# The down projection of a hybrid decoder step, its order written by hand and its last two column tiles taken together in three token parts

## Chip, cores and metric

The kernel runs on one core of one Trainium2 chip. A time is the device time of one execution in microseconds (us). The core has five engines that work beside each other: TensorE (PE; its loads of the stationary operand are listed as PEld), VectorE (DVE), ScalarE (ACT), GpSimd (POOL) and SyncE (SP), which here only issues DMAs. The profile takes one execution apart by instruction.

## The reference, cut to what matters

The kernel is one step of a one-layer decoder trunk for a prompt of 512 tokens and 8 single sample tokens, which are worked on together as 520 columns. The change concerns the last part of the layer:

```python
x = layer_norm(ALPHA * x + mixed @ w_out, ln1_g, ln1_b)         # D_MODEL = 1024
g, u = jnp.split(x @ w_gate_up, 2, axis=-1)                     # D_FF = 2816
ffn = (jax.nn.silu(g) * u) @ w_down                             # (520 x 2816) @ (2816 x 1024)
ple = jax.nn.sigmoid(x @ w_ple_gate) * (p @ w_ple)
x = layer_norm(ALPHA * x + ffn + ple, ln2_g, ln2_b)             # y_prompt, y_sample
```

## The kernel before

Activations are kept with the features on the 128 partitions and the 520 tokens as columns: 8 sample tokens first, then 512 prompt tokens. A matrix product in float32 accuracy is made of three products of rounded parts: each weight and each activation is split into a part hi and a remainder lo, and hi x hi, hi x lo and lo x hi are summed in PSUM. A weight piece is split by two instructions in `split` (L215): a copy to hi on ScalarE (L216) and a subtraction for lo on VectorE (L217).

Weights come through three rings. `add_block` registers blocks of a weight matrix in the order of use, each cut into pieces. `load_next` (DMA at L163, on SyncE's queue) brings a block into one of two `raw` buffers of 128 x 2048. `prep_next` splits the next piece into the rings `whi` and `wlo` of three buffers each, or into a place named in `dest`; when a block's last piece is split, the next load is issued. `get(k)` prepares pieces up to k + 2 and hands out piece k.

The down projection has 8 output tiles of 128 features (f = 0 to 7) and 22 blocks of 128 along D_FF (k). In the kernel before, tiles 0 to 5 are made in three pairs (b); for each pair there are three groups of k (8, 8 and 6) and two pieces, one per tile, so 18 pieces. `mm3ab` (matmuls at L243) takes each piece against both token halves, 264 and 256 columns, in two PSUM banks: for each k and each of the three products two matmuls follow each other with the same stationary weights. Tile 6 has three pieces of its own and the same form. Tile 7 is made by halves: first `mm3` (L226) for the 264 columns, then `mmb` (L1843) for the 256 columns.

Beside this runs the end of the layer. `mkbase(f)` forms ALPHA * x + ple for tile f: per half, two loads that SyncE issues (L1748 for the saved tanh `th`, from a ring of three, and L1749 for the saved `ple` product) and three VectorE instructions (L1750 to L1752). A finished half tile is added to its base from PSUM (`ev_d`, L1776), transposed to tokens on partitions by two TensorE transposes (`ev_dt`, L1785), copied to the row buffer R2 by ScalarE (L1786), and its statistics are taken by VectorE (`ev_ds`, L1794).

Around tiles 0 to 6 the order of instructions on each engine is the framework's: it simulates a timeline and picks. From the second half of tile 7 on, the order is written out by hand (`tc.manual_schedule` for TensorE, VectorE, GpSimd and ScalarE; the DMA queue of SyncE is left to the framework). In that last part the tokens of chunks 0 and 1 are normalised while `mmb` runs, those of chunks 2 and 3 after it: per chunk of 128 tokens the mean and variance (L1858, L1859), a power on GpSimd (L1860), then centering times gain (L1867) and scaling plus shift (L1871) on VectorE; for three quarters of the second chunk of each pair it is a normalisation on ScalarE (L1875), the gain on GpSimd (L1879) and the shift on VectorE (L1883). Stores are issued at L1887. The 8 sample tokens are normalised with their features on partitions (L1902 to L1928), transposed at L1940 and stored.

Of the kernel before, what the change touches and what calls it, by code (L numbers as in the profile page):

```python
# [17 lines left out]
P = 128  # L18
D = 1024
KD = D // P  # L20
NS = 8
# [24 lines left out]
def rr(ap):  # L46
    return ap.bitcast(F32R)
# [3 lines left out]
def tile_hybrid_step(  # L51
# [25 lines left out]
    def psm():  # L77
        return pm.tile([P, 512], F32, tag="m", name=nm("psm"))
# [7 lines left out]
    def ring(tag, n, bufs, p=P):  # L86
        return wp.tile([p, n], F32, tag=tag, name=nm(tag), bufs=bufs)
# [3 lines left out]
    def slab(i):  # L91
        return up.tile([P, U], F32, tag=f"T{i}", name=nm(f"T{i}_"))
# [94 lines left out]
    def prep_next():  # L187
        i = state["prep"]
        if i >= len(pieces):
            return  # L190
        state["prep"] += 1
        bi_, a, kc, pcol, last = pieces[i]
# [5 lines left out]
        split(hi, lo, raws[bi_][:, :, a : a + pcol], G if i in pool_lo else V)  # L198
        ready[i] = (hi, lo)
        if last:  # L200
            raws.pop(bi_)
            load_next()
# [1541 lines left out]
    def mkbase(f):  # L1744
        for hf, (c0, n) in enumerate(HALVES):
            th = ring("th", 264, 3)[:, :n]
            bs = base(f, hf)
            nc.sync.dma_start(th, thsc[:, f, c0 : c0 + n])  # L1748
            nc.sync.dma_start(bs, plesc[:, f, c0 : c0 + n])  # L1749
            V.scalar_tensor_tensor(bs, th, 1.0, bs, ALU.add, ALU.mult)  # L1750
# [19 lines left out]
    def dpart(g, w):  # L1770
        return [(w[0], w[1], 0, KG[g][1], hhi[g], hlo[g], 0)]
# [24 lines left out]
    kp = k_dn  # L1796
    for b in range(3):
        pps = [(psm(), psm()) for _ in range(2)]
        cnt = [0, 0]
        for g in range(3):  # L1800
            for a in range(2):
                w = get(kp)
                kp += 1
                i = 6 * b + 2 * g + a
                for j in range(2 * i, 2 * i + 2) if i < 3 else ():
                    split(hhi[2][j], hlo[2][j], h6[j])
                for j in bases.get(i, ()):
                    mkbase(j)
                if i == 12:
                    late_rows()  # L1810
                cnt[a] = mm3ab(pps[a], dpart(g, w), total=3 * KF, begin=cnt[a])
                if g == 2:
                    if "R2" not in late_r:
                        late_r["R2"] = slab(2)[:, : NCH * D].rearrange("p (c d) -> p c d", c=NCH)
                    for hf in range(2):
                        f = 2 * b + a
                        ev_ds(f, hf, ev_dt(f, hf, ev_d(f, hf, pps[a][hf])))
    pp = (psm(), psm())
    cnt = 0
    for g in range(3):  # L1820
        w = get(kp)
        kp += 1
        cnt = mm3ab(pp, dpart(g, w), total=3 * KF, begin=cnt)
    for hf in range(2):
        ev_ds(6, hf, ev_dt(6, hf, ev_d(6, hf, pp[hf])))
    pa, pb = psm(), psm()
    ws = []
    cnt = 0
    for g in range(3):
        ws.append(get(kp, 1))  # L1830
        kp += 1
        cnt = mm3(pa, HALVES[0], dpart(g, ws[g]), total=3 * KF, begin=cnt)

    R2 = late_r["R2"]
    ysm, l2g, l2b, RQ, rss = (late_r[n] for n in ("ysm", "g", "b", "RQ", "rss"))
    h0, h1, q3 = slice(0, 512), slice(512, D), slice(768, D)

    def mmb(k0, k1):
        for k in range(k0, k1):
            g, j = k // 8, k % 8  # L1840
            hi, lo = ws[g]
            for i, (w, x) in enumerate(((hi, hhi), (hi, hlo), (lo, hhi))):
                T.matmul(  # L1843
                    pb[:, :256], rr(w[:, j, :]), rr(x[g][j][:, 264:NT]),
                    start=(k == 0 and i == 0), stop=(k == KF - 1 and i == 2),
                )

    class Out:
        def __init__(self, c):
            self.c = c  # L1850
            self.mv = ring("mv2", 4, 2).rearrange("p (k a) -> p k a", k=2)
            self.rs = ring("rs2", 2, 2)
            self.nb = ring("nb", 1, 2)
            self.r = [R2[:, c + i, :] for i in range(2)]

        def stats(self):
            for i in range(2):
                V.bn_aggr(self.mv[:, i, :], st2[:, self.c + i])  # L1858
            V.tensor_scalar(self.rs, self.mv[:, :, 1], LN_EPS, None, ALU.add)  # L1859
            G.tensor_tensor(self.rs, self.rs, nhalf[:, :2], ALU.pow)  # L1860

        def neg(self):
            V.scalar_tensor_tensor(self.nb, self.mv[:, 1, 0:1], -1.0, self.rs[:, 1:2], ALU.mult, ALU.mult)

        def center(self, i, cs):
            s = self.r[i][:, cs]
            V.scalar_tensor_tensor(s, s, self.mv[:, i, 0:1], l2g[:, cs], ALU.subtract, ALU.mult)  # L1867

        def scale(self, i, cs):
            s = self.r[i][:, cs]  # L1870
            V.scalar_tensor_tensor(s, s, self.rs[:, i : i + 1], l2b[:, cs], ALU.mult, ALU.add)  # L1871

        def norm(self, a):
            s = self.r[1][:, a : a + 256]
            S.activation(s, s, AF.Identity, bias=self.nb, scale=self.rs[:, 1:2])  # L1875

        def gain(self, a):
            s = self.r[1][:, a : a + 256]
            G.tensor_tensor(s, s, l2g[:, a : a + 256], ALU.mult)  # L1879

        def shift(self, a):
            s = self.r[1][:, a : a + 256]
            V.tensor_tensor(s, s, l2b[:, a : a + 256], ALU.add)  # L1883

        def store(self, i, cs, eng=nc.sync):
            t0 = (self.c + i) * P
            eng.dma_start(y_prompt[0, t0 : t0 + P, cs], self.r[i][:, cs])  # L1887
# [7 lines left out]
    E = mybir.EngineType  # L1895
    with tc.manual_schedule(engines={E.PE, E.DVE, E.Pool, E.Activation}):
        oa, ob = Out(0), Out(2)
        r2a = ev_d(7, 0, pa)
        mmb(0, 4)
        psa = ev_dt(7, 0, r2a)  # L1900
        pst = pss()
        T.matmul(pst[:, :64], onesD, RS.rearrange("p f b -> p (f b)"), start=True, stop=True)  # L1902
        mmb(4, 10)
# [3 lines left out]
        ev_ds(7, 0, psa)  # L1907
        oa.stats()
        T.matmul(pst[:, 64:128], onesD, RQ.rearrange("p f b -> p (f b)"), start=True, stop=True)
        mmb(10, KF)  # L1910
        oa.center(0, h0)
        V.tensor_reduce(rss[:, 1], pst[:, 64:128].rearrange("p (f b) -> p b f", f=KD), axis=AX.X, op=ALU.add)
        V.tensor_scalar(rss[:, 1], rss[:, 1], LN_EPS, None, ALU.add)
        G.tensor_tensor(rss[:, 1], rss[:, 1], nhalf[:, 0:1].to_broadcast([P, NS]), ALU.pow)
        oa.neg()
        for a in range(0, 768, 256):
            oa.norm(a)
            oa.gain(a)
        oa.scale(0, h0)
        oa.store(0, h0)  # L1920
        oa.center(0, h1)
        oa.scale(0, h1)
        oa.store(0, h1)
        oa.center(1, q3)
        oa.shift(0)
# [3 lines left out]
        r2b = ev_d(7, 1, pb)  # L1929
        psb = ev_dt(7, 1, r2b)  # L1930
        oa.scale(1, q3)
        oa.shift(256)
        oa.store(1, h0)
        oa.shift(512)
        oa.store(1, h1)
        ev_ds(7, 1, psb)
        ob.stats()
# [6 lines left out]
        ob.center(0, h0)  # L1944
        ob.neg()
        for a in range(0, 768, 256):
            ob.norm(a)
        for a in range(0, 768, 256):
            ob.gain(a)
        ob.scale(0, h0)  # L1950
        ob.store(0, h0)
        ob.center(1, q3)
        ob.scale(1, q3)
        ob.center(0, h1)
        ob.shift(0)
        ob.scale(0, h1)
        ob.store(0, h1)
        ob.shift(256)
        ob.store(1, h0, nc.scalar)
        ob.shift(512)  # L1960
        ob.store(1, h1)
# [33 lines left out]
```

## Time and profile before

| | us |
|---|---|
| median of 3 runs | 891.84 |
| lowest and highest run | 890.12, 892.92 |
| the profiled execution | 894.93 |
| its span, first to last instruction | 892.9 |

The profile is of one execution; its span is 2.0 us shorter than its time. Rows of the profile give times from the start of the span. The granted clock is that of TensorE, as a share of 2.4 GHz.

### The profile page before, as it was taken

The numbers are of one execution on the slowest core, as the hardware profiler recorded it, in microseconds if no ns is written. First come the engines' busy times: TensorE is split into PE (matmuls) and PEld (weight loads), VectorE is DVE, ScalarE is ACT, GpSimd is POOL, SyncE is SP. The second block draws the span as 40 slices with busy tenths as digits, with TensorE's granted clock in tenths as the row PEclk, the third lists the DMA queues.
The fourth block names the chain that finished last, engine by engine and source line by source line (L and its number), as shares of the span: only waits on it lengthen the run. The fifth ranks groups of instructions, "written<-read, shape, count | busy, mean of one in ns | idle before, by whom it ended". The sixth has DMA issues, their size and how long they took to land.

```text
span 892.9 us, 18610 instructions
## 1 busy us (share of the span) xinstructions
PE 866.8 (97%) x7082; PEld 854.0 (96%) x7082; DVE 658.9 (74%) x1591; ACT 480.6 (54%) x1138; POOL 160.5 (18%) x320
## 2 busy tenths in 40 slices
PE   8899999999999999999999999999999999999994
PEld 7899899999999899999999999999999999999993
DVE  6797655688878777778877879899988875824327
ACT  5545354657777655557426646666666565212212
POOL 4441321115364411311013200000000000000004
PEclk9999999999999999999999999999999999999997
DMA  7543631336465451121610223334333348641212
GB/s 241 176 156 104 170 122 54 56 120 149 144 177 162 143 142 49 50 93 48 231 54 1 73 85 105 107 96 118 107 96 107 108 123 255 197 161 61 69 40 96
DMA packets 128089, 103.69 MB, mean 116 GB/s; under 512 B 7242, under 2 KB 123682, under 8 KB 127976
## 3 DMA queue, kind: packets, MB, share of 16 engines
q1 hardware_dynamic: 127856, 102.25, 38.4%
q8 instruction: 55, 0.90, 0.4%
q14 instruction: 34, 0.28, 0.1%
q10 hardware_dynamic: 144, 0.26, 0.1%
HBM read 91.14 MB, written 12.47 MB: 116 GB/s over the span
## 4 chain that ended last, share of the span: by engine, by line
PE 77%; DVE 10%; DMA 5%; ACT 3%; issue 2%; POOL 1%; SPq 1%; DVEq 0%; ACTq 0%; POOLq 0%
PE psm L243 36%; PE psm L1600 14%; PE pss L1600 10%; PE psm L226 6%; DMA big<-vsd 2%; DVE wlo L217 1%; PE pss L736 1%; PE psm L467 1%; PE pss L683 1%; PE pss L720 1%; PE psm L1428 1%; DMA thsc<-gt 1%; DMA wdb<-bcd 1%; ACT T L1371 1%; PE pss L1069 1%
## 5 line engine op out<-in xcount | busy, mean ns | idle before, releaser
L243 PE MATMUL psm<-T,whi 128*128 128x264 f32 (+1 forms) x1744 | 304.3, 286 | 0.7 <-DVE Qbd L670 0.4
L243 PEld LDWEIGHTS psm<-T,whi 128*128 128x128 f32 x1744 | 248.5, 188 | 2.9 <-issue 0.8
L243 PE MATMUL psm<-T,wlo 128*128 128x256 f32 (+1 forms) x928 | 203.2, 288 | 2.0 <-DVE wlo L217 2.0
L217 DVE TENSOR_TENSOR wlo<-raw,whi 128x1024 fp32r<-128x1024 f32 (+1 forms) x78 | 94.6, 1213 | 76.0 <-ACT whi L216 75.3
L243 PEld LDWEIGHTS psm<-T,wlo 128*128 128x128 f32 x928 | 147.8, 188 | 3.1 <-DVE wlo L217 2.5
L216 ACT ACTIVATE whi<-raw 128x1024 fp32r<-128x1024 f32 (+1 forms) x78 | 80.6, 1035 | 120.6 <-PE psm L243 108.4
L1778 POOL COPY amaskA<-tmp 128x8 f32<-128x8 f32 x8 | 1.7, 207 | 372.7 <-DVE tmp L1776 372.7
L708 POOL TENSOR_SCALAR g<-g,sm 128x256 f32<-128x256 f32 (+1 forms) x64 | 36.4, 582 | 80.5 <-DVE sm L706 24.1
L1584 DVE TENSOR_TENSOR whi<-raw,whi 128x512 fp32r<-128x512 f32 x55 | 37.8, 687 | 11.7 <-ACT whi L1579 10.8
L243 PE MATMUL psm<-L,whi 128*128 128x264 f32 x224 | 45.4, 282 | 0.0
L1579 ACT ACTIVATE whi<-raw 128x512 fp32r<-128x512 f32 x55 | 34.5, 628 | 19.4 <-PE psm L1600 14.4
L1579 ACT ACTIVATE wlo<-raw 128x512 fp32r<-128x512 f32 x55 | 34.6, 629 | 16.2 <-ACT gt L1618 10.1
L1584 DVE TENSOR_TENSOR wlo<-raw,wlo 128x512 fp32r<-128x512 f32 x55 | 37.7, 686 | 6.0 <-ACT wlo L1579 5.6
L701 ACT ACTIVATE g<-g,sm 128x256 f32<-128x256 f32 (+1 forms) x64 | 30.2, 474 | 18.9 <-DVE sm L697 17.8
L1600 PE MATMUL psm<-tf,whi 128*128 128x260 f32 x276 | 36.7, 281 | 0.0
L217 POOL TENSOR_TENSOR gt<-big,gt 128x256 fp32r<-128x256 f32 x32 | 27.4, 866 | 50.7 <-ACT gt L216 32.1
L1600 PE MATMUL psm<-T,wlo 128*128 128x260 f32 x264 | 35.3, 283 | 0.0
L1600 PE MATMUL pss<-tf,whi 128*128 128x260 f32 x264 | 35.3, 283 | 0.0
L1600 PE MATMUL pss<-tf,wlo 128*128 128x260 f32 x264 | 35.3, 283 | 0.0
L1600 PE MATMUL psm<-T,whi 128*128 128x260 f32 x264 | 35.3, 283 | 0.0
L243 PEld LDWEIGHTS psm<-L,whi 128*128 128x128 f32 x224 | 34.6, 188 | 0.0
L1600 PEld LDWEIGHTS psm<-tf,whi 128*128 128x128 f32 x276 | 34.5, 188 | 0.0
(448 smaller groups left out, 2090.6 us busy)
## 6 DMA issues: line engine op xcount, KB each, us to landing
raw<-in_w_in_dram SPq DMA_DIRECT2D x24, 1024.0 KB
raw<-in_w_gate_up_dram SPq DMA_DIRECT2D x72, 256.0 KB
raw<-in_w_down_dram SPq DMA_DIRECT2D x6, 1024.0 KB
big<-in_state_mlstm_C_dram SPq DMA_DIRECT2D x8, 512.0 KB
big<-vsd SPq DMA_DIRECT2D x8, 512.0 KB
out_dram<-big SPq DMA_DIRECT2D x8, 512.0 KB
raw<-in_w_out_dram SPq DMA_DIRECT2D x4, 1024.0 KB
raw<-in_w_gate_up_dram SPq DMA_DIRECT2D x4, 1024.0 KB
```

Source lines behind the costliest of these rows:

```text
L216: S.activation(rr(hi), src, AF.Copy)
L217: (le or V).tensor_tensor(rr(lo), src, hi, ALU.subtract)
L226: T.matmul(ps[:, :n], rr(w[:, k, wc : wc + P]), rr(a[k0 + k][:, c0 : c0 + n]), start=(i == 0), stop=(i == tot - 1),)
L243: T.matmul(ps[:, :n], rr(w[:, k, wc : wc + P]), rr(a[k0 + k][:, c0 : c0 + n]), start=(i == 0), stop=(i == tot - 1),)
L467: T.matmul(t01[t][hf][:, :n], rr(w[:, k, :]), rr(x[k][:, c0 : c0 + n]), start=(k == 0 and i == 0), stop=(k == KD - 1 and i == 2),)
L683: T.matmul(sc[:, a, :w], rr(q[:, a, n * P : (n + 1) * P]), rr(KS[:, kv, hl, (n - 1 + k0) * P : (n + 1) * P]), start=(hl == 0), stop=(hl == 1),
L701: S.activation(pr[:, a, :w], pr[:, a, :w], AF.Exp, bias=sm[:, 2 + a : 3 + a], scale=ASC, accum_out=sm[:, 8 + a : 9 + a],)
L708: G.tensor_scalar(pr[:, a, :w], pr[:, a, :w], sm[:, 12 + a : 13 + a], 0.5, ALU.mult, ALU.mult)
L720: T.transpose(pt[:, b, a, :], pr[:, a, b * P : (b + 1) * P], ident)
L1579: S.activation(rr(t[:, 0]), wsrcs[i], AF.Copy)
L1584: V.tensor_tensor(rr(lo), wsrcs.pop(i), hi, ALU.subtract)
L1600: T.matmul(ps[:, :TH], rr(w[:, j, :]), rr(x[j]), start=(start and j == 0 and i == 0), stop=(j == 3 and i == 2), skip_group_check=not start,)
```

## The change

The whole down projection up to the end of the kernel now stands in one hand-ordered block. For tiles 0 to 5 each of the 18 steps of the loop lists, in this order: the adds of a tile that was finished in the step before, the splits of the piece two steps ahead, the statistics of the tile before, the base of a tile (loaded one step ahead by the new `load_base`), the matmuls, and only then the transposes and copies of the finished tile.

Tiles 6 and 7 are made together. Their weights come as three blocks of 256 columns (two of 8 k, one of 6), cut along k into six pieces of 4, 4, 4, 4, 4 and 2 k, all of which are kept; three of them go to places that are free by then (`dest`). The tokens are taken in three parts. The first part (8 sample tokens and chunks 0 and 1, 264 columns) is made as before with weights stationary, for both tiles, into two banks. The other two parts are chunks 2 and 3: in `mmc` the activations h (128 k x 128 tokens) are stationary and 256 weight columns move, so that the result has tokens on partitions; the bases of tiles 6 and 7 for these tokens are transposed into R2 ahead of it, and `ev_c` adds the result to them in place. Chunk 2 is normalised while the matmuls of chunk 3 run. The normalisation is now on VectorE alone, in 512-wide steps. The transposes of the sample rows stand between the matmuls of chunk 3.

```diff
-    def add_block(src, kc, ncol, pcol=P):
+    def add_block(src, kc, ncol, pcol=P, kstep=KD):
...
-        for a in range(0, ncol, pcol):
-            pieces.append((bi_, a, kc, pcol, a + pcol >= ncol))
+        for k0 in range(0, kc, kstep):
+            kn = min(kstep, kc - k0)
+            for a in range(0, ncol, pcol):
+                pieces.append((bi_, a, k0, kn, pcol, a + pcol >= ncol and k0 + kn == kc))
...
-    for f in (6, 7):
-        for k0, kc in KG:
-            add_block(w_dn2[k0 * P : (k0 + kc) * P, P * f : P * (f + 1)], kc, P)
+    for k0, kc in KG:
+        add_block(w_dn2[k0 * P : (k0 + kc) * P, 768:], kc, 256, 256, 4)
...
-    def mkbase(f):
+    def load_base(f):
+        ths = []
         for hf, (c0, n) in enumerate(HALVES):
-            th = ring("th", 264, 3)[:, :n]
+            ths.append(ring("th", 264, 3)[:, :n])
+            nc.sync.dma_start(ths[-1], thsc[:, f, c0 : c0 + n])
+            nc.sync.dma_start(base(f, hf), plesc[:, f, c0 : c0 + n])
+        return ths
...
-    bases = {2: (0,), 3: (1,), 5: (2,), 6: (3,), 7: (4,), 8: (5,), 9: (6,), 10: (7,)}
+    BASES = (2, 3, 6, 7, 8, 9, 10, 11)
...
     with tc.manual_schedule(engines={E.PE, E.DVE, E.Pool, E.Activation}):
+        done, trs, ths = None, None, {}
+        for i in range(18):
+            b, g, a = i // 6, i % 6 // 2, i % 2
+            if done:
+                f, ps2 = done
+                r2s = [ev_d(f, hf, ps2[hf]) for hf in range(2)]
+            if i % 6 == 0:
+                pps = [(psm(), psm()) for _ in range(2)]
+                cnt = [0, 0]
+            w = get(k_dn + i)
+            if trs:
+                for hf in range(2):
+                    ev_ds(trs[0], hf, trs[1][hf])
+                trs = None
+            for j in range(2 * i, 2 * i + 2) if i < 3 else ():
+                split(hhi[2][j], hlo[2][j], h6[j])
+            if i in BASES:
+                f = BASES.index(i)
+                mkbase(f, ths.pop(f))
+            if i + 1 in BASES:
+                f = BASES.index(i + 1)
+                ths[f] = load_base(f)
+            if i == 12:
+                late_rows()
+                w0 = slab(0)
+                dsts = [f256(w0[:, 1024 * k :]) for k in range(4)]
+                dsts += [f256(slab2(k, "w5")[1]) for k in (2, 3)]
+                for k in range(3):
+                    dest[k_dn + 18 + k] = dsts[2 * k], dsts[2 * k + 1]
+            cnt[a] = mm3ab(pps[a], dpart(g, w), total=3 * KF, begin=cnt[a])
+            if done:
+                trs = done[0], [ev_dt(done[0], hf, r2s[hf]) for hf in range(2)]
+            done = (2 * b + a, pps[a]) if g == 2 else None
+
+        ws = []
+        r2s = [ev_d(5, hf, done[1][hf]) for hf in range(2)]
+        pA = psm(), psm()
+        hk = [(hhi[k // 8][k % 8], hlo[k // 8][k % 8]) for k in range(KF)]
+        for q in range(6):
+            ws.append(get(k_dn + 18 + q))
...
+            for j in range(4 * q, min(4 * q + 4, KF)):
+                hi, lo = (t[:, j % 4, :] for t in ws[q])
+                xh, xl = hk[j]
+                for a in range(2):
+                    for i, (w, x) in enumerate(((hi, xh), (hi, xl), (lo, xh))):
+                        T.matmul(
+                            pA[a][:, :264], rr(w[:, a * P : (a + 1) * P]), rr(x[:, :264]),
+                            start=(j == 0 and i == 0), stop=(j == KF - 1 and i == 2),
+                        )
...
+        def mmc(c, k0, k1):
+            t0 = NS + (2 + c) * P
+            for k in range(k0, k1):
+                hi, lo = (t[:, k % 4, :] for t in ws[k // 4])
+                for i, (w, x) in enumerate(((hi, 0), (hi, 1), (lo, 0))):
+                    T.matmul(
+                        pC[c][:, :256], rr(hk[k][x][:, t0 : t0 + P]), rr(w),
+                        start=(k == 0 and i == 0), stop=(k == KF - 1 and i == 2),
+                    )
+
+        def ev_c(c):
+            r = R2[:, 2 + c, q3]
+            V.tensor_tensor(r, pC[c][:, :256], r, ALU.add)
+            for a in range(2):
+                V.bn_stats(st2[:, 2 + c, 6 + a, :], R2[:, 2 + c, 768 + a * P : 768 + (a + 1) * P])
...
+        mmc(1, 0, 14)
         ysp = [pss(), pss()]
         for f in range(KD):
             T.transpose(ysp[f // 4][:NS, (f % 4) * P : (f % 4 + 1) * P], RS[:, f, :], ident)
+        mmc(1, 14, KF)
...
+        for cs in (h0, h1):
+            ob.center(0, cs)
+            ob.scale(0, cs)
+            ob.store(0, cs)
+        ev_c(1)
+        oc.stats()
+        oc.center(0, h0)
+        oc.center(0, h1)
+        oc.scale(0, h0)
+        oc.store(0, h0)
+        oc.scale(0, q2)
+        oc.store(0, q2, nc.scalar)
+        oc.scale(0, q3)
+        oc.store(0, q3)
```

The last group of stores and scalings before (`ob`) worked on chunks 2 and 3 together; in the new code `oa` has chunks 0 and 1, `ob` chunk 2 and `oc` chunk 3.

## Rows read from the trace of the kernel before

**Rows 1.** The page, busy us, share of the span, count.
```profile
PE 866.8 (97%) x7082; PEld 854.0 (96%) x7082; DVE 658.9 (74%) x1591; ACT 480.6 (54%) x1138; POOL 160.5 (18%) x320
```
**Rows 2.** Table of stretches, columns as in its first line.
```profile
core 0: us, PE busy (x) PEld busy (x) DVE busy (x) ACT busy (x) POOL busy (x), PEclk, DMA share, GB/s
...
745.50:777.00 31.50, 31.32 (x259) 31.11 (x259) 26.15 (x60) 9.92 (x15) 0.00 (x0) 1.00 0.74 226
777.00:861.40 84.40, 83.62 (x699) 83.63 (x700) 28.75 (x57) 19.48 (x28) 1.27 (x6) 1.00 0.29 91
```
**Rows 3.** Timeline of TensorE, 736 to 790: its rows with idle time before.
```profile
745.53 0.51 PE L243 MATMUL psm<-T,wlo 128*128 128x264 f32 x2 [0.51 <-DVE wlo L217]
...
777.78 0.44 PE L1785 MATMUL pss<-ident,tmp 128*128 128x128 f32 x2 [0.93 <-DVE tmp L1776]
```
**Rows 4.** Timeline, 877.5 to 884.6: start us, us, engine, line.
```profile
878.07 0.28 PE L1843 MATMUL psm<-h,wlo 128*128 128x256 f32 x1
878.47 0.94 DVE L1883 TENSOR_TENSOR T<-T,T 128x256 f32<-128x256 f32 x1
...
879.84 0.23 DVE L1928 TENSOR_TENSOR amaskA<-amaskA,vecs 128x64 f32<-128x64 f32 x1
879.98 0.41 DVE L1776 TENSOR_TENSOR tmp<-psm,stg 128x256 f32<-128x256 f32 x1
...
880.79 1.04 PE L1940 MATMUL pss<-ident,amaskA 128*8 128x128 f32 x8
...
881.41 0.49 DVE L1794 BATCH_NORM_STATS2 amaskA<-pss 128x6 f32<-128x128 f32 x2
...
881.82 0.58 DVE L1858 BATCH_NORM_AGGREGATE mv<-amaskA 128x2 f32<-128x48 f32 x2
...
882.44 0.17 DVE L1859 TENSOR_SCALAR rs<-mv 128x2 f32<-128x2 f32 x1
882.51 0.74 DVE L1867 SCALAR_TENSOR_TENSOR T<-T,mv,T 128x512 f32<-128x512 f32 x1
...
882.69 1.13 POOL L1860 TENSOR_TENSOR rs<-rs,nhalf 128x2 f32<-128x2 f32 x1 [3.55 <-DVE rs L1859]
...
883.92 0.74 DVE L1871 SCALAR_TENSOR_TENSOR T<-T,rs,T 128x512 f32<-128x512 f32 x1
```
**Rows 5.** Timeline, 884.5 to 890.
```profile
884.72 2.92 POOL L1879 TENSOR_TENSOR T<-T,T 128x256 f32<-128x256 f32 x3 [0.91 <-ACT T L1875]
...
885.85 1.21 DVE L1867 SCALAR_TENSOR_TENSOR T<-T,mv,T 128x512 f32<-128x512 f32 x1
...
888.51 0.74 DVE L1883 TENSOR_TENSOR T<-T,T 128x256 f32<-128x256 f32 x2
```
**Rows 6.** The chain that ended last: start us, us, what, how many.
```profile
815.86 27.20 PE psm L243 x227
...
864.73 5.12 PE psm L226 x42
...
869.85 1.41 PE psm L1843 x12
```
**Rows 7.** Groups by line and form, 745 to 878.4: busy us, mean ns.
```profile
L217 DVE TENSOR_TENSOR wlo<-raw,whi 128x1024 fp32r<-128x1024 f32 x16 | 19.5, 1221 | 28.8 <-ACT whi L216 28.4
```
**Rows 8.** The chain, 755 to 780.
```profile
759.77 1.02 DVE h L1751 x3
...
761.54 3.89 DMA gt<-plesc
```
**Rows 9.** Timeline of SyncE's queue and of ScalarE, 735 to 744.
```profile
735.83 0.39 SPq L163 DMA_DIRECT2D raw<-in_w_down_dram  x1
...
743.15 1.06 ACT L216 ACTIVATE whi<-raw 128x1024 fp32r<-128x1024 f32 x1 [2.88 <-DMA raw<-in_w_down_dram]
```
**Rows 10.** Table of half microseconds at the end; the last figure is GB/s.
```profile
891.00:891.50 0.50, 0.00 (x0) 0.00 (x0) 0.00 (x0) 0.00 (x0) 0.00 (x0) 0.50 0.88 336
891.50:892.00 0.50, 0.00 (x0) 0.00 (x0) 0.00 (x0) 0.00 (x0) 0.00 (x0) 0.50 0.00 0
```

More of the change, by code (lines that the diff above doesn't have):

```diff
@@ L191, in prep_next @@
         state["prep"] += 1
-        bi_, a, kc, pcol, last = pieces[i]
+        bi_, a, k0, kc, pcol, last = pieces[i]
         if i in dest:
@@ L197, in prep_next @@
             lo = ring("wlo", 1024, 3)[:, : kc * pcol].rearrange("p (k n) -> p k n", k=kc)
-        split(hi, lo, raws[bi_][:, :, a : a + pcol], G if i in pool_lo else V)
+        split(hi, lo, raws[bi_][:, k0 : k0 + kc, a : a + pcol], G if i in pool_lo else V)
         ready[i] = (hi, lo)
@@ L1794, in ev_ds @@
             V.bn_stats(st2[:, 2 * hf + i, f, :], ps[:, i * P : (i + 1) * P])
[L1796 to L1887, printed above, removed]
@@ L1889, in wide @@
+    R2 = slab(2)[:, : NCH * D].rearrange("p (c d) -> p c d", c=NCH)
+    late_r["R2"] = R2
+    q0, q1, q2, q3 = (slice(a, a + 256) for a in range(0, D, 256))
+    h0, h1 = slice(0, 512), slice(512, D)
     def wide(v):
@@ L1893, in col, with f256, __init__, stats @@
         return vecs[:, o : o + KD].unsqueeze(2).to_broadcast([P, KD, NS])
-    E = mybir.EngineType
-    with tc.manual_schedule(engines={E.PE, E.DVE, E.Pool, E.Activation}):
[L1897 to L1900, printed above, removed]
+    def f256(t):
+        return t[:, :1024].rearrange("p (k n) -> p k n", k=4)
+    class Out:
+        def __init__(self, c, n=1):
+            self.c, self.n = c, n
+            self.mv = ring("mv2", 4, 3).rearrange("p (k a) -> p k a", k=2)
+            self.rs = ring("rs2", 2, 3)
+        def stats(self):
+            n = self.n
+            for i in range(n):
+                V.bn_aggr(self.mv[:, i, :], st2[:, self.c + i])
+            rs = self.rs[:, :n]
+            V.tensor_scalar(rs, self.mv[:, :n, 1], LN_EPS, None, ALU.add)
+            G.tensor_tensor(rs, rs, nhalf[:, :n], ALU.pow)
+        def center(self, i, cs):
+            s = R2[:, self.c + i, cs]
+            V.scalar_tensor_tensor(s, s, self.mv[:, i, 0:1], late_r["g"][:, cs], ALU.subtract, ALU.mult)
+        def scale(self, i, cs):
+            s = R2[:, self.c + i, cs]
+            V.scalar_tensor_tensor(s, s, self.rs[:, i : i + 1], late_r["b"][:, cs], ALU.mult, ALU.add)
+        def store(self, i, cs, eng=nc.sync):
+            t0 = (self.c + i) * P
+            eng.dma_start(y_prompt[0, t0 : t0 + P, cs], R2[:, self.c + i, cs])
@@ new lines, in tile_hybrid_step @@
+    with tc.manual_schedule(engines={E.PE, E.DVE, E.Pool, E.Activation}):
+        done, trs, ths = None, None, {}
[37 more added lines that the diff above has]
+            ws.append(get(k_dn + 18 + q))
+            if q == 0:
+                for hf in range(2):
+                    ev_ds(trs[0], hf, trs[1][hf])
+            if q == 2:
+                for hf in range(2):
+                    ev_ds(5, hf, trs[hf])
+            for j in range(4 * q, min(4 * q + 4, KF)):
[7 more added lines that the diff above has]
+                        )
+            if q == 0:
+                trs = [ev_dt(5, hf, r2s[hf]) for hf in range(2)]
+            if q == 3:
+                ps = pss()
+                for c in range(2):
+                    for a in range(2):
+                        T.transpose(
+                            ps[:, (2 * c + a) * P : (2 * c + a + 1) * P],
+                            base(6 + a, 1)[:, c * P : (c + 1) * P], ident,
+                        )
+                S.activation(R2[:, 2:4, q3], ps.rearrange("p (c d) -> p c d", c=2), AF.Copy)
+        ysm, RQ, rss = (late_r[n] for n in ("ysm", "RQ", "rss"))
+        pC = [psm(), psm()]
+        def mmc(c, k0, k1):
[6 more added lines that the diff above has]
+                        start=(k == 0 and i == 0), stop=(k == KF - 1 and i == 2),
+                    )
+        def ev_c(c):
+            r = R2[:, 2 + c, q3]
+            V.tensor_tensor(r, pC[c][:, :256], r, ALU.add)
+            for a in range(2):
+                V.bn_stats(st2[:, 2 + c, 6 + a, :], R2[:, 2 + c, 768 + a * P : 768 + (a + 1) * P])
+        oa, ob, oc = Out(0, 2), Out(2), Out(3)
+        r2s = [ev_d(6 + a, 0, pA[a]) for a in range(2)]
+        mmc(0, 0, 4)
+        pt = [ev_dt(6 + a, 0, r2s[a]) for a in range(2)]
@@ L1901, in tile_hybrid_step @@
         pst = pss()
         T.matmul(pst[:, :64], onesD, RS.rearrange("p f b -> p (f b)"), start=True, stop=True)
-        mmb(4, 10)
+        mmc(0, 4, 14)
+        for a in range(2):
+            ev_ds(6 + a, 0, pt[a])
+        oa.stats()
         V.tensor_reduce(rss[:, 0], pst[:, :64].rearrange("p (f b) -> p b f", f=KD), axis=AX.X, op=ALU.add)
@@ L1906, in tile_hybrid_step @@
         V.tensor_tensor(RQ, RS, RS, ALU.mult)
-        ev_ds(7, 0, psa)
-        oa.stats()
         T.matmul(pst[:, 64:128], onesD, RQ.rearrange("p f b -> p (f b)"), start=True, stop=True)
-        mmb(10, KF)
+        mmc(0, 14, KF)
         oa.center(0, h0)
+        oa.center(0, h1)
         V.tensor_reduce(rss[:, 1], pst[:, 64:128].rearrange("p (f b) -> p b f", f=KD), axis=AX.X, op=ALU.add)
@@ L1914, in tile_hybrid_step @@
         G.tensor_tensor(rss[:, 1], rss[:, 1], nhalf[:, 0:1].to_broadcast([P, NS]), ALU.pow)
[L1915 to L1918, printed above, removed]
         oa.scale(0, h0)
         oa.store(0, h0)
-        oa.center(0, h1)
         oa.scale(0, h1)
         oa.store(0, h1)
-        oa.center(1, q3)
-        oa.shift(0)
+        oa.center(1, h0)
         V.tensor_tensor(RS, RS, wide(rss[:, 1]), ALU.mult)
@@ L1928, in tile_hybrid_step @@
         V.tensor_tensor(RS, RS, col(V_L2B), ALU.add)
[L1929 to L1932, printed above, removed]
+        ev_c(0)
+        ob.stats()
+        oa.scale(1, h0)
         oa.store(1, h0)
-        oa.shift(512)
+        oa.center(1, h1)
+        oa.scale(1, h1)
         oa.store(1, h1)
-        ev_ds(7, 1, psb)
-        ob.stats()
+        mmc(1, 0, 14)
         ysp = [pss(), pss()]
@@ L1943, in tile_hybrid_step @@
         nc.sync.dma_start(y_sample[:, 0, :], ysm)
[L1944 to L1961, printed above, removed]
+        for cs in (h0, h1):
[12 more added lines that the diff above has]
+        oc.store(0, q3)
 _INS = ['x_prompt', 'x_sample', 'state_mlstm_C', 'state_mlstm_n', 'state_mlstm_m', 'state_conv',
```

6 lines of the change are left out of this document (3 added, 3 removed).

## The prediction

> **What bounds the kernel now.** I read the page's busy lines first, then the table of stretches, the waits of TensorE, the chain, and last the timeline of the final 25 us. TensorE is busy 97% of the span [rows 1], and in the down projection it is busy almost without a hole: 31.32 of 31.50 us in the first stretch and 83.62 of 84.40 in the long one behind it, at a granted clock of 1.00, the 2.4 GHz level [rows 2]. Whatever else the change touches there (splits, bases, DMAs) is work beside TensorE and counts only where it makes TensorE wait. The waits it has now are few: 0.51 us for the first split weights, and 0.93 us at 777.78, where the transposes of the first finished tile stand in TensorE's queue until VectorE has added the base to it [rows 3].
>
> The other bounded place is the end. The last matmul starts at 878.07 and takes 0.28, so it ends at 878.35 [rows 4]; the span ends at 892.9. These 14.55 us have no matmul of weight in them. The reader should see three parts. VectorE is late: the add that takes the last result out of PSUM starts only at 879.98, 1.63 us after the matmul, because older normalisation stands before it (a gain-shift step of 0.94 and three small ones from 878.47 on). Then add, transposes, statistics and the power on GpSimd run until 883.92. Then VectorE normalises two 128-token chunks until 889.25, and the stores need 3.65 us more [rows 4, 5]. TensorE's length up to its last matmul, plus this tail, is the time; so the sum has those two terms.
>
> **The change part by part: matmuls.** Tiles 0 to 5 keep their 792 matmuls. Tiles 6 and 7 had 22 x 3 x 2 halves x 2 tiles = 264; the new form has 132 of 264 columns (first part, both tiles) and 2 x 66 of 256 columns (the last two parts, h stationary). So 132 of each width before and after. Their pace: 227 alternating ones in 27.20 us, 0.120 each; 42 of 264 columns, each with a stationary operand of its own, in 5.12 us, 0.122; 12 of 256 in 1.41, 0.1175 [rows 6]. A wide one and a narrow one with separate loads cost 0.2395 together, two that share a stationary operand 0.240. I price the regrouping at nothing. Bounds: below nothing is excluded, as the columns are the same; above, if a load of 128x128 were exposed it would cost its own time, and no row shows one exposed.
>
> Rows show tile 7 at full pace without any reuse of the stationary operand [rows 6]. [...] The sum goes by the rows.
>
> **Transposes.** Moved ahead of the last matmul are the eight small transposes of the sample rows, 1.04 us together [rows 4], and two of tile 7's second half, 0.13 each by the same row. TensorE's length grows by 1.3 (bounds 0.9 to 1.3, the low one if they run at the pace of half a 256-column matmul).
>
> **The hand order, tiles 0 to 5.** The transposes of a finished tile now stand behind the next piece's matmuls (4 to 5.7 us) and the add stands first in VectorE's iteration, so the 0.93 us wait goes (bounds 0 and 1.4, with the 0.51 too; I take 0.9, since the first split is due to a load outside the edit). The price could be new waits: VectorE now runs the bases in program order. One iteration of 48 matmuls lasts 48 x 0.12 = 5.7 us; VectorE has one split of 1.22, six base steps of 0.34 and, at tile ends, two adds of 0.41 and four statistics [rows 4, 7, 8]: at most 5.5 us. The split of piece i+2 is done some 2.3 us into iteration i (1.06 on ScalarE, 1.22 on VectorE [rows 7, 9]) and is needed at 11.4, so a wait in front of it is covered up to about 9 us. A load of a base half takes up to 3.9 us to land [rows 8], and it is issued an iteration ahead. I price this at nothing. The ring of three th buffers makes every second load wait for the first base step of the tile before; 3.9 us plus an issue is still below an iteration. SyncE's queue: the raw loads are three of 1 MB, 1 MB and 768 KB in place of six, each due at least two pieces later; one of 1 MB was issued at 735.83 and its split began at 743.15, 7.3 us [rows 9], and two pieces ahead there is 8.5. Cover enough; without it 1 to 2 us on TensorE.
>
> **The tail.** Chunk 2 now leaves TensorE 66 matmuls (7.8 us) before chunk 3, and chunk 3 comes with tokens on partitions. So after the last matmul there remain (durations of [rows 4]): hand-over 0.1, an add of 256 columns 0.41, two statistics 0.49, one aggregation 0.29 (half of 0.58), 0.17; then the power, 1.31 from the end of the small step (882.61) to the first scaling (883.92), with two centerings of 0.74 over it, 1.48, which decides; then scalings of 0.74, 0.41 and 0.41. Sum 4.5; VectorE's steps overlap by some 0.07 each, so I take 4.4 (4.0 to 4.8). Transposes, the PSUM copy on ScalarE, and the second chunk's normalisation are gone from it. Behind the last VectorE step stood 3.65 us, in which data flowed until about 891.5 [rows 5, 10]: three stores of 256 KB. Now 256, 128 and 128 KB are left, the first 0.8 us earlier. At most 3.65; at least 1.4 (the part after the data) plus an issue and 128 KB, some 2.3. I take 2.9. New tail 4.4 + 2.9 = 7.3 (6.4 to 8.4); gain 14.55 - 7.3 = 7.25.
>
> This needs VectorE free when the last matmul ends. From the end of the first part to there TensorE needs 132 x 0.1175 + 4 transposes 0.5 + 8 more 1.04 + two column sums, 17.2 us. VectorE in that time: two adds 0.82, four statistics 0.98, aggregation 0.75, twelve 512-wide steps 8.9, chunk 2's add and statistics 0.9 and aggregation 0.46, eight small steps of 0.23 1.8: 14.6, plus 1.3 idle before the first transposes. 15.9, so 1.3 in hand.
>
> The row with the power at 882.69 shows a centering beside it at its normal 0.74, and rows with wide GpSimd products show 1.21 instead [rows 4, 5]; the change drops these products. The Trainium skill (GPSIMD Engine Reference, 8. Key points) says that GpSimd shares its SBUF interfaces with VectorE instructions of two SBUF inputs. Applied to the power too, the two centerings would take 2.4 and the tail be 0.9 longer; by the row it is not.
>
> **Sum.** -0.9 + 1.3 - 7.25 = -6.85. The profiled execution took 894.93 (span 892.9 and 2.0 around it), 3.1 above the median; its counterpart is 888.1. The terms are absolute, so against the median: 891.84 - 6.85 = 885.0.
>
> **Rivals.**
> (A) VectorE becomes the bound of the last part. For it: it has only 1.3 us in hand, and ScalarE and GpSimd no longer help with the normalisation. Against: the products that slowed it are gone. At 0.1 us of hand-over for each of 30 steps it is 3.0 - 1.3 = 1.7 late, and if the stores still take 3.65, the gain is 6.85 - 1.7 - 0.75 = 4.4: 887.4.
> (B) The hand order makes TensorE wait a little in several places, at ring slots, late raw loads, adds. For it: the old order had only 1.44 us of such waits, and little can get better. Against: the covers above. Six waits of 1 us: 890.9.
> (C) Other side: VectorE stands in its fixed order at a base step whose th load is queued behind a 1 MB raw load that itself waits for a split. Price: 7.3 + 3.9 = 11.2 us against a cover of 9, 2.2 us of TensorE each time [rows 8, 9]. It decides from 3.2 strikes on; at the six bases of iterations 6 to 11 it costs 13.2: 898.2. Against: the load is issued an iteration ahead, and the raw queue stands still only every second piece.
> (D) The change doesn't shorten TensorE's side because the h-stationary matmuls cost more: 0.052 us more on each of 132 is enough to reach 891.8. Against: tile 7's pace [rows 6].
>
> **How the numbers follow.** Forecast 0.70, A 0.13, B 0.08, C 0.06, D 0.03. A measurement of this kernel tells some 0.3% (2.7 us) from no change: faster is below 889.2, slower above 894.5. Forecast and A are faster, with a sliver of B: 0.84. B and most of D are within: 0.09. C and the rest: 0.07. The forecast's own range is 883.3 (tail 6.4, both waits gone, transposes 0.9) to 887.1 (tail 8.4, no wait gone). With A, the start of B and the spread of the three runs (890.12 to 892.92) it is 882.3 to 889.0, which leaves out B's rest, C, D and a little below.
>
> **What would show it.** Right: TensorE's busy share in the down projection as now, no wait at transposes of tile 0, the last matmul within 1 us of where it is, an add of 256 columns from PSUM within 0.2 us of it, about 4.4 us of VectorE after, and some 7.3 from the last matmul to the end. Wrong: the add late (A), waits for wlo or whi on TensorE (B), VectorE idle before base steps (C), a pace above 0.122 in the last 132 matmuls (D).

## Result and profile after

The changed kernel takes 885.6 us (median of 5 runs, 883.25 to 886.79); beside runs of the kernel before on the same chip the ratio is 0.9924, with a 95% interval of 0.9897 to 0.9952. Forecast were 885.0 and a range of 882.3 to 889.0. A second set of runs gave 0.9927 (0.9901 to 0.9954). One execution of the kernel before, of 4804.67 us, is left out of the ratio. The profiled execution took 885.6 with a span of 883.5.

The page's busy line answers to [rows 1], the stretches to [rows 2]:

```profile
PE 866.0 (98%) x7082; PEld 853.2 (97%) x7082; DVE 659.4 (75%) x1589; ACT 475.5 (54%) x1131; POOL 156.2 (18%) x315
```

```profile
745.50:775.00 29.50, 29.50 (x248) 29.50 (x247) 15.68 (x26) 8.94 (x13) 0.19 (x1) 1.00 0.59 190
775.00:858.00 83.00, 83.00 (x695) 83.00 (x694) 40.43 (x86) 19.11 (x29) 0.95 (x5) 1.00 0.33 107
858.00:876.10 18.10, 18.10 (x154) 17.73 (x153) 13.56 (x34) 1.72 (x4) 4.05 (x5) 1.00 0.24 90
876.10:880.50 4.40, 0.01 (x1) 0.00 (x0) 4.21 (x10) 0.00 (x0) 0.99 (x1) 0.75 0.00 0
880.50:883.50 3.00, 0.00 (x0) 0.00 (x0) 0.00 (x0) 0.00 (x0) 0.00 (x0) 0.50 0.48 175
```

TensorE has no hole from the first stretch to its last matmul; the stretch behind that has VectorE in it and one power on GpSimd, and the last one only the stores. In the chain that ended last (start, us, what, how many), TensorE stands without a break:

```profile
746.40 29.84 PE psm L245 x249
776.25 0.44 PE pss L1791 x4
776.68 5.78 PE psm L245 x48
...
854.33 4.37 PE psm L1894 x36
858.71 1.44 PE psm L1918 x12
...
864.53 7.86 PE psm L1918 x66
872.39 0.87 PE pss L1967 x8
873.26 2.86 PE psm L1918 x24
```

The transposes of tile 0 stand at 776.25 with no wait before them; this is where 0.93 us were lost [rows 3]. The h-stationary matmuls (L1918) run at 7.86 / 66 = 0.119 us each.

The tail in the timeline answers to [rows 4, 5], and the table of half microseconds to [rows 10]:

```profile
875.83 0.28 PE L1918 MATMUL psm<-wlo,h 128*128 128x256 f32 x1
876.14 0.42 DVE L1925 TENSOR_TENSOR T<-psm,T 128x256 f32<-128x256 f32 x1 [1.69 <-PE psm L1918]
876.60 0.49 DVE L1927 BATCH_NORM_STATS2 amaskA<-T 128x6 f32<-128x128 f32 x2
877.13 0.37 DVE L1825 BATCH_NORM_AGGREGATE mv<-amaskA 128x2 f32<-128x48 f32 x1
877.53 0.15 DVE L1827 TENSOR_SCALAR rs<-mv 128x1 f32<-128x1 f32 x1
877.60 1.40 DVE L1832 SCALAR_TENSOR_TENSOR T<-T,mv,T 128x512 f32<-128x512 f32 x2
877.76 0.99 POOL L1828 TENSOR_TENSOR rs<-rs,nhalf 128x1 f32<-128x1 f32 x1 [7.32 <-DVE rs L1827]
878.92 1.53 DVE L1836 SCALAR_TENSOR_TENSOR T<-T,rs,T 128x512 f32<-128x512 f32 x3
```

```profile
881.50:882.00 0.50, 0.00 (x0) 0.00 (x0) 0.00 (x0) 0.00 (x0) 0.00 (x0) 0.50 0.90 307
882.00:882.50 0.50, 0.00 (x0) 0.00 (x0) 0.00 (x0) 0.00 (x0) 0.00 (x0) 0.50 0.00 0
```

The add follows the last matmul's end (875.83 + 0.28 = 876.11) by 0.03 us, after VectorE had waited 1.69 for it. VectorE ends at 880.45, 4.3 after the matmul; the span ends 3.05 later. The tail is 883.5 - 876.11 = 7.39 us, where it was 14.55.

The two spans differ by 9.4 us, more than the medians do, and the reader should not credit it all to the change. A mark that both kernels share is the last product of the stage before (twelve matmuls of 260 columns, between the first pieces of the down projection). It starts at 746.96 in the trace of before and at 744.81 here. What lies ahead of it is the same code, but for the first matmuls of the down projection and the wait for the first split weights [rows 3], and across the traces of this study it starts anywhere between 742.9 and 747.0. From the mark on, the profile can be divided:

| trace | mark | last matmul ends | between | tail | sum from the mark |
|---|---|---|---|---|---|
| before | 746.96 | 878.35 | 131.39 | 14.55 | 145.94 |
| change | 744.81 | 876.11 | 131.30 | 7.39 | 138.69 |
| change, second profile | 745.34 | 876.65 | 131.31 | 7.35 | 138.66 |
| old end | 743.51 | 874.66 | 131.15 | 14.54 | 145.69 |
| new end only | 745.31 | 877.34 | 132.03 | 7.36 | 139.39 |
| two parts | 745.97 | 876.75 | 130.78 | 11.15 | 141.93 |
| old end, VectorE only | 744.96 | 876.25 | 131.29 | 14.25 | 145.54 |
| two more VectorE steps | 743.60 | 874.90 | 131.30 | 7.40 | 138.70 |
| six more VectorE steps | 742.93 | 874.24 | 131.31 | 9.86 | 141.17 |
| GpSimd products beside | 743.38 | 874.69 | 131.31 | 8.51 | 139.82 |
| samples late | 745.28 | 875.67 | 130.39 | 7.33 | 137.72 |
| samples late, again | 744.66 | 875.06 | 130.40 | 7.34 | 137.74 |

From the mark the change is worth 145.94 - 138.69 = 7.25 us, and 7.2 of them are the tail. The column "between", TensorE's section, repeats to some 0.02 us where the code is the same, the tails to 0.05 (spans are printed to 0.1), the times only to a few us.

### The profile page after: what moved, and what is told of

The parts are those of the page before. It is cut to its first block, busy times and chain, and to the rows that moved or that the text cites. A ratio compares the mean times of both kernels' runs of the same rounds, so it can differ in the third digit from the quotient of the medians.

```text
span 883.5 us, 18583 instructions
## 1 busy us (share of the span) xinstructions
PE 866.0 (98%) x7082; PEld 853.2 (97%) x7082; DVE 659.4 (75%) x1589; ACT 475.5 (54%) x1131; POOL 156.2 (18%) x315
## 4 chain that ended last, share of the span: by engine, by line
PE 87%; DVE 5%; DMA 3%; ACT 2%; issue 1%; POOL 1%; SPq 0%; DVEq 0%; ACTq 0%
PE psm L245 41%; PE psm L1601 14%; PE pss L1601 11%; PE psm L228 5%; PE psm L1894 2%; PE psm L1918 2%; PE pss L684 2%; PE pss L737 1%; PE pss L721 1%; PE psm L1429 1%; DMA big<-vsd 1%; PE psm L468 1%; PE pss L1070 1%; PE pss L1074 1%; DMA wdb<-bcd 1%
## 5 line engine op out<-in xcount | busy, mean ns | idle before, releaser
L245 PE MATMUL psm<-T,wlo 128*128 128x256 f32 (+1 forms) x912 | 200.1, 288 | 1.5 <-DVE wlo L219 1.5
L245 PEld LDWEIGHTS psm<-T,wlo 128*128 128x128 f32 x912 | 145.7, 189 | 2.5 <-DVE wlo L219 1.9
L219 DVE TENSOR_TENSOR wlo<-raw,whi 128x1024 fp32r<-128x1024 f32 (+2 forms) x75 | 90.5, 1207 | 66.8 <-ACT whi L218 66.7
L218 ACT ACTIVATE whi<-raw 128x1024 fp32r<-128x1024 f32 (+2 forms) x75 | 77.2, 1034 | 96.9 <-PE psm L245 79.5
L245 PE MATMUL psm<-L,whi 128*128 128x264 f32 x192 | 38.7, 282 | 0.0
L1601 PE MATMUL psm<-tf,wlo 128*128 128x260 f32 x252 | 33.5, 282 | 0.0
```

Source lines behind the costliest of these rows:

```text
L245: T.matmul(ps[:, :n], rr(w[:, k, wc : wc + P]), rr(a[k0 + k][:, c0 : c0 + n]), start=(i == 0), stop=(i == tot - 1),)
L1601: T.matmul(ps[:, :TH], rr(w[:, j, :]), rr(x[j]), start=(start and j == 0 and i == 0), stop=(j == 3 and i == 2), skip_group_check=not start,)
```

## Experiments

**Old end.** The hand-ordered loop is kept and led on through tile 6 and the first half of tile 7; the blocks, `Out` and everything from `mmb` on are those of before. The edit is shown against the change.

```diff
-        for i in range(18):
-            b, g, a = i // 6, i % 6 // 2, i % 2
+        for i in range(24):
+            b, g, a = (i // 6, i % 6 // 2, i % 2) if i < 18 else (3, i % 3, i // 21)
...
+            if i < 21:
+                cnt[a] = mm3ab(pps[a], dpart(g, w), total=3 * KF, begin=cnt[a])
+            else:
+                ws.append(w)
+                cnt[a] = mm3(pa, HALVES[0], dpart(g, w), total=3 * KF, begin=cnt[a])
```

> Hand order for tiles 0 to 6 and the first half of tile 7, but the old end: tile 7 by halves with weights stationary, two chunks normalised together with help of ScalarE and GpSimd. Theory (the gain is the end): the transposes of tile 0 no longer make TensorE wait, worth 0.9 to 1.2 us, and from the last matmul to the end of the span it takes 14.5 us as before; time about 891, within 0.3% of before. Rival (the gain is the hand order and the regrouped weights): about 886, with the last matmul several us earlier than before.

Measured: 891.07 us (12 runs) against 892.63, ratio 0.9988 (0.9973 to 1.0003); tail 14.54. The wait at tile 0 is gone, but TensorE's section fell by only 0.24, because another wait came. TensorE's rows with idle time before them, from 840 on:

```profile
867.26 0.44 PE L1790 MATMUL pss<-ident,tmp 128*128 128x128 f32 x2 [0.60 <-DVE tmp L1781]
876.76 0.44 PE L1790 MATMUL pss<-ident,tmp 128*128 128x128 f32 x2 [2.11 <-DVE tmp L1781]
```

This kernel has two hand-ordered blocks, the loop and the old end, and the framework mixes one into the other: twelve matmuls of the second half of tile 7 (L1850) ran before the first half (L226) was complete, and were then missing as cover between its add and its transposes. In the chain:

```profile
863.07 0.83 PE psm L1850 x7
863.89 0.25 PE psm L226 x2
864.14 0.59 PE psm L1850 x5
864.73 1.95 PE psm L226 x16
```

That belongs to this edit, not to the change. The wait at 876.76 is the old tail's late add. The hand order alone doesn't carry the gain.

**New end only.** Tiles 0 to 5 are written as before, outside the hand-ordered block; from the first part of tiles 6 and 7 on it is the change. The edit is shown against the change.

```diff
-        for i in range(18):
...
-            if done:
-                f, ps2 = done
-                r2s = [ev_d(f, hf, ps2[hf]) for hf in range(2)]
...
+                if g == 2:
...
+                    for hf in range(2):
+                        f = 2 * b + a
+                        ev_ds(f, hf, ev_dt(f, hf, ev_d(f, hf, pps[a][hf])))
+    R2 = late_r["R2"]
+    with tc.manual_schedule(engines={E.PE, E.DVE, E.Pool, E.Activation}):
```

> Tiles 0 to 5 in the framework's order as before, tiles 6 and 7 and the end as in the change. Theory (the gain is the end): from the last matmul to the end 7.4 us; TensorE waits about 1 us for the transposes of tile 0 again; time about 886.5, 1 us above the change. Rival (the hand order carries it): the last matmul several us later than in the change, 890 or more.

Measured: 887.63 us (9 runs, 886.35 to 891.32), ratio 0.9956 (0.9937 to 0.9975); tail 7.36. TensorE's section is 0.73 longer than the change's, and its one wait behind the mark is the old one:

```profile
775.76 0.44 PE L1786 MATMUL pss<-ident,tmp 128*128 128x128 f32 x2 [0.56 <-DVE tmp L1777]
```

So the new end brings the whole tail by itself. The trace puts this kernel 6.55 us under before, its interval 2.2 to 5.6; the profiled execution (886.83) was the third of its nine from below. What else the framework's order costs no trace shows.

**Samples late.** The eight transposes of the sample rows go behind the last matmul.

```diff
-        mmc(1, 0, 14)
+        mmc(1, 0, KF)
         ysp = [pss(), pss()]
...
-        mmc(1, 14, KF)
```

> The change with the eight transposes of the sample rows put behind the last matmul in place of between matmuls. Theory (TensorE's length up to the last matmul plus the tail is the time): the last matmul ends 0.87 us earlier, the add follows it at once, the tail stays 7.4 us, since the sample rows' copies and store (some 4.5 us) fit in it; time 0.9 us below the change. Rival (the transposes cost nothing where they are, or the sample store then ends last): no gain, within 0.2 us of the change, or up to 1 us slower.

Measured: 884.78 us (6 runs), ratio 0.9918 (0.9895 to 0.9941); TensorE's section 130.39, 0.91 less than the change's, and tail 7.33. Run once more beside the change itself:

> The change itself, beside the next run on the same chip. Theory: as measured first, 0.992 of before; from the last matmul to the end 7.4 us; no wait for transposes in the tiles' loop, and the wait for the first split weights between 0 and 0.5 us by chance.

> The sample rows' transposes behind the last matmul, beside the change on the same chip. Theory: 0.87 us less between the last product of the stage before and the last matmul, tail 7.4 us, so 0.9 us (0.1%) below the change, which the medians may just show. Rival: no difference.

Measured: the change 885.9 us, ratio 0.9927; samples late 886.9, ratio 0.9937 (0.9915 to 0.996). The section is 130.40 against 131.31 and the tails are 7.34 and 7.35, so the 0.91 us are there in both traces; in the medians of 6 runs, which spread by 3 to 6 us, they are not. The change's second profile had the wait for the first split weights (0.5 us) that its first had not, as expected.

```profile
874.78 0.28 PE L1918 MATMUL psm<-wlo,h 128*128 128x256 f32 x1
874.89 1.03 PE L1967 MATMUL pss<-ident,amaskA 128*8 128x128 f32 x8
...
875.09 0.42 DVE L1925 TENSOR_TENSOR T<-psm,T 128x256 f32<-128x256 f32 x1 [0.79 <-PE psm L1918]
```

In the timeline of this last run the transposes stand beside VectorE's tail. VectorE's wait for the last matmul is 0.79 in place of 1.69: the 0.9 came out of its slack.

**Two parts.** Tiles 6 and 7 together, but the last 256 tokens in one part with weights stationary; adds, transposes and copies after the last matmul, then two chunks on VectorE.

```diff
+        def mmb(k0, k1):
             for k in range(k0, k1):
                 hi, lo = (t[:, k % 4, :] for t in ws[k // 4])
-                for i, (w, x) in enumerate(((hi, 0), (hi, 1), (lo, 0))):
-                    T.matmul(
-                        pC[c][:, :256], rr(hk[k][x][:, t0 : t0 + P]), rr(w),
...
+                for a in range(2):
+                    for i, (w, x) in enumerate(((hi, 0), (hi, 1), (lo, 0))):
+                        T.matmul(
+                            pB[a][:, :256], rr(w[:, a * P : (a + 1) * P]), rr(hk[k][x][:, 264:NT]),
...
```

> The change with the last 256 tokens of tiles 6 and 7 in one part, weights stationary, results with features on partitions: both tiles are added to their bases, transposed and copied after the last matmul, and two chunks are normalised there, all on VectorE without wide GpSimd products. Matmuls are as many and as wide. Theory (h stationary saves the transposes and, by finishing chunk 2 earlier, one chunk of normalisation): the tail is 12 us in place of 7.4, time about 890. Rival (the gain comes from VectorE being free at the last matmul and from dropping the GpSimd products, not from the token parts): tail under 9.5 us, time under 888.

Measured: 887.92 us (6 runs), ratio 0.9947 (0.9927 to 0.9967); tail 11.15. Its timeline:

```profile
876.43 0.78 DVE L1782 TENSOR_TENSOR tmp<-psm,stg 128x256 f32<-128x256 f32 x2 [5.69 <-PE psm L1909]
876.47 0.28 PE L1909 MATMUL psm<-h,wlo 128*128 128x256 f32 x1
877.00 0.70 PE L1791 MATMUL pss<-ident,tmp 128*128 128x128 f32 x4 [0.26 <-DVE tmp L1782]
877.45 0.67 ACT L1792 ACTIVATE T<-pss 128x256 f32<-128x256 f32 x2 [2.88 <-PE pss L1791]
877.86 0.89 DVE L1800 BATCH_NORM_STATS2 amaskA<-pss 128x6 f32<-128x128 f32 x4 [0.66 <-ACT T L1792]
...
880.70 1.42 DVE L1836 SCALAR_TENSOR_TENSOR T<-T,rs,T 128x512 f32<-128x512 f32 x2
...
883.35 1.54 DVE L1836 SCALAR_TENSOR_TENSOR T<-T,rs,T 128x512 f32<-128x512 f32 x3
```

VectorE is free here too (it waited 5.69 us), yet the tail is 3.8 us longer than the change's. The first scaling starts 1.1 later after the last matmul's end (3.95 against 2.81): 0.6 for the transposes and copies ahead of the statistics, 0.5 for statistics and aggregations of two chunks in place of one. From there to VectorE's end it is 4.19 in place of 1.53, 2.7 more, for the four wide steps of the second chunk.

The rival's bound on the tail, 9.5, is passed; its bound on the time, 888, is not (887.92), and the time of 890 that the theory named is missed. In the medians this kernel lies some 2 us behind the change, from the mark 3.2. The token parts earn 3.8 of the 7.2 in the tail, but part of it is paid on TensorE: its section is 0.52 shorter here, 0.44 of it the four transposes of the bases, which only the change has (L1904).

**Old end, VectorE only.** In the kernel before, `norm`, `gain` and the small step `neg` that `norm` needed do nothing, and `shift(0)` makes both steps over the 768 columns on VectorE.

```diff
         def norm(self, a):
-            s = self.r[1][:, a : a + 256]
-            S.activation(s, s, AF.Identity, bias=self.nb, scale=self.rs[:, 1:2])
+            pass
...
         def shift(self, a):
-            s = self.r[1][:, a : a + 256]
-            V.tensor_tensor(s, s, l2b[:, a : a + 256], ALU.add)
+            if a == 0:
+                self.center(1, slice(0, 768))
+                self.scale(1, slice(0, 768))
```

> The kernel before with the normalisation of all four chunks on VectorE alone: no ScalarE normalisation and no wide GpSimd products; the old token halves, order and stores stay. Theory (the old tail is long because two chunks and the transposes stand behind the last matmul): VectorE's steps go back to 0.74 per 512 columns, but it has more of them; the tail falls from 14.5 us to about 14.0, time within 0.3% of before. Rival (the wide GpSimd products made the tail long, and dropping them is the gain of the change): tail under 12 us, time under 889.5.

Measured: 892.86 us (10 runs) against 892.27, ratio 1.0014 (0.9991 to 1.0037); tail 14.25.

```profile
875.97 0.28 PE L1843 MATMUL psm<-h,wlo 128*128 128x256 f32 x1
...
877.90 0.42 DVE L1776 TENSOR_TENSOR tmp<-psm,stg 128x256 f32<-128x256 f32 x1
...
885.05 1.68 DVE L1871 SCALAR_TENSOR_TENSOR T<-T,rs,T 128x768 f32<-128x768 f32 x2
```

The add is still 1.65 us late. To give the helpers' share to VectorE, at its faster pace, is worth 0.3 in the tail and nothing in the times.

**VectorE's slack.** More 512-wide steps on spare data just before the last add, two in the first kernel and six in the second; they are additions, nothing is left out.

```diff
+        for _ in range(2):
+            V.scalar_tensor_tensor(late_r["pad"], late_r["g"][:, h0], 1.0, late_r["b"][:, h0], ALU.mult, ALU.add)
         ev_c(1)
```

> The change with two more 512-wide VectorE steps on spare data just before the add that takes chunk 3 out of PSUM. Theory (VectorE has 1.7 us in hand there): they end at the last matmul, the add starts within 0.15 us of it, tail 7.4 us as in the change. Rival A (VectorE is the bound of the last part): the add is 1.4 us late, tail 8.8.

> The same with six such steps, 6 x 0.70 = 4.2 us. Theory: 4.2 - 1.7 = 2.5 us late, tail 9.9 us, so the point from which VectorE decides lies at 1.7 us. If VectorE had no slack, 4.2 late and tail 11.6; if the power or the stores hid it, tail under 9.

Measured, one execution each: 884.39 us, tail 7.40, the add 0.04 after the last matmul; and 886.17 us, tail 9.86. The timeline of the second, from 874 on, so that its first row has the last four of the six steps:

```profile
873.95 2.87 DVE L1978 SCALAR_TENSOR_TENSOR T<-T 128x512 f32<-128x512 f32 x4
873.96 0.28 PE L1919 MATMUL psm<-wlo,h 128*128 128x256 f32 x1
...
876.73 0.41 DVE L1926 TENSOR_TENSOR T<-psm,T 128x256 f32<-128x256 f32 x1
```

The matmul ends at 874.24 and the add starts 2.49 later, by which the tail is longer: VectorE decides from 1.7 us of extra work on, as the 1.69 of waiting in the change's own trace says.

**GpSimd products beside.** Three products of 128 x 256 on spare data behind the last power.

```diff
         oc.stats()
+        for _ in range(3):
+            G.tensor_tensor(late_r["pad"][:, :256], late_r["g"][:, q0], late_r["b"][:, q0], ALU.mult)
```

> The change with three GpSimd products of 128 x 256 on spare data behind the power of the last chunk, so that they run beside VectorE's last scalings; their results are not used. If wide GpSimd products slow VectorE as in the old end, the three last scalings take 2.4 to 2.7 us in place of 1.53 and the tail is about 8.4 us. If the slow steps of the old end had another cause, they stay at 1.53 and the tail at 7.4.

Measured, one execution: 885.32 us, tail 8.51.

```profile
877.30 2.85 POOL L1980 TENSOR_TENSOR T<-T 128x256 f32<-128x256 f32 x3
877.50 2.94 DVE L1837 SCALAR_TENSOR_TENSOR T<-T,rs,T 128x512 f32<-128x512 f32 x3
```

The scalings take 2.94 in place of 1.53, with the same operands. With the kernel before on VectorE only, where such steps are back at 0.75 per 512 columns, this shows that the slow steps of the old end came from the products beside them. The tail grows by 1.12, less than the 1.41 of the scalings.

## Why the prediction was right, step by step

**The place and the size.** The two terms were TensorE's length to its last matmul and the tail. Forecast were +0.4 and -7.25, together -6.85; from the mark the trace shows -0.09 and -7.16, together -7.25, and the times 0.9924, some -6.8. One sign named in advance, the last matmul within 1 us of where it was, holds only from the mark: on the span's own clock it ends 2.2 earlier, by what lies ahead.

**The tail** was forecast as 4.4 us of VectorE and 2.9 of stores, and measured 4.3 and 3.05. The single steps were within 0.1 of the rows that priced them. What earned it is shown by a series of tails: 14.55 as before; 14.25 with VectorE alone; 11.15 with both tiles together and VectorE free at the last matmul; 7.39 with the last two parts h stationary. The step from 14.25 to 11.15 changes several things at once: 1.65 is the late add, and 0.76 the stores behind VectorE's last step (3.77 against 3.01), of which the last two are half as big; the remaining 0.7 isn't split further. In the last step, the layout (no transposes and copies, 0.6) and the earlier finish of chunk 2 (3.2) are told apart by the rows of one trace, not by runs of their own. The hand order of tiles 0 to 5 does nothing for it (14.54 with the old end, 7.36 without the hand order).

**TensorE's term** was mis-sized by half a microsecond. The transposes moved ahead cost 0.87 + 0.22, and 0.91 came back when the eight were moved away; 1.3 was too much, since 1.04 in [rows 4] is the duration of a group to its last result, while the next matmul starts earlier. The wait of 0.93 [rows 3] was worth more than its idle time. The matmul ahead of it in the trace of before:

```profile
776.57 0.28 PE L243 MATMUL psm<-h,wlo 128*128 128x264 f32 x1
```

The transposes start 1.21 after this start (777.78), where matmuls here follow each other by 0.12: 1.09 lost, as idle is counted from the modelled end of that matmul, and the next one would have started before this end. The kernel with only the new end confirms it: there 0.56 of idle goes with a section 0.73 longer. With 1.09 won and 1.09 spent, TensorE's term is nothing, to 0.09. The wait of 0.51, which lies ahead of the mark, was rightly left out of the change: it comes and goes (none in the change's first profile and in the framework-ordered kernel with VectorE only, 0.5 in the change's second). Some small sums of the prediction are off, without weight: the ends of the forecast's own range come to 883.2 and 887.0, rival B to 891.0, and ten transposes at half the pace of a 256-column matmul to 0.6 and not 0.9.

**Matmuls priced at nothing.** The h-stationary ones run at 0.119 against 0.1175 [rows 6], which were only twelve. The kernel with two parts has weights stationary in the same places: its 66 matmuls between the second column sum and the sample rows' transposes take 7.83 us, the change's 7.89. Rival D falls.

The prediction speaks of a reuse of the stationary operand in the old order, and the trace shows none. PE and PEld have the same count, x7082 in both kernels [rows 1]: each matmul has a load of its own, also where two in a row name the same piece of weights, as in the last matmuls of before:

```profile
877.72 0.31 PEld L1843 LDWEIGHTS psm<-h,whi 128*128 128x128 f32 x2
877.83 0.40 PE L1843 MATMUL psm<-h,whi 128*128 128x256 f32 x2
```

So the regrouping had nothing to lose, and whether a load that is really saved would make a matmul faster no run shows. No load is exposed at this pace. The Trainium skill (TensorE: Matmul & The Clock Gate, Part 2, Step-by-step) says that the weights of the next tile load while the matmul of this one runs; the trace agrees, with 0.119 us per matmul and a load for each.

**VectorE's hand.** Forecast 1.3 us, 1.69 measured, and two experiments put the point of decision there. Rival A falls for this kernel, but not by much. **Rivals B and C.** TensorE waits for nothing in the hand-ordered loop but the first split weights, and VectorE's waits from 738 on name no load at all, so the cover of two pieces was enough.

**GpSimd.** The Trainium skill's rule (GPSIMD Engine Reference, 8. Key points) that GpSimd shares its SBUF interfaces with VectorE agrees with the trace for wide products (2.94 against 1.53 us); beside the power nothing of it shows: the two centerings took 1.40, and two without GpSimd in the kernel with two parts 1.41. The forecast weighed it rightly, for the power. Dropping the products gave only 0.3 in the old tail, where VectorE then has the helpers' steps to do; in the new tail three such products cost 1.12.

**Open:** the hand order is worth 0.7 us by the trace without it, but the two medians lie 2 us apart, and the intervals of the two ratios overlap; the times can't settle this.

## What to carry to other kernels

At the end of a kernel, ask which operand is stationary: with activations stationary the result comes out with tokens on partitions, needs no transpose behind the last matmul, and can be finished part by part, so that only the last part's normalisation stands behind the last matmul. Count what the last engine has in hand when the last matmul ends, since that, not its busy share, says when it decides. A wait on TensorE can cost more than the idle time shown for it: compare the starts. Compare spans from a mark behind which the code differs; what lies ahead of it moved by 4 us here from one execution to the next.

## What the runs showed of the hardware

Three GpSimd products of 128 x 256, 0.95 us each, almost doubled VectorE's two-input steps while they ran (2.94 against 1.53 us for 1024 columns); a power over one column per partition beside the same kind of step cost it nothing (two in 1.40). TensorE's eight transposes of 128 x 8 hold it for 0.87 us in the chain, though as a group they last 1.04. Each matmul has a load of its own (both x7082), also where two in a row name the same stationary operand; at 256 columns the load hides behind the matmuls, which follow each other by 0.119 us with h and with weights stationary.
